# Stack loads of the forgetting stage: alternate partitions and partitions 32 to 95 instead of halves

## Chip, cores and metric

One core of a Trainium2 chip runs a whole decoder layer in float32. The metric is the device time of one execution in microseconds; before the change it is 1514.79 us, the median of three runs (1514.67 to 1516.5).

## What is computed

The layer runs two groups of heads on the same normalised input, an mLSTM (4 heads of 128) and a forgetting attention (8 heads of 64). Their outputs are joined and projected; a cross-attention and an MLP with squared ReLU follow. The change lies in the forgetting attention. For one head, with queries q, keys k, values v, and c the running sum of its log forget gates:

```python
s = jnp.einsum('bqhd,bkhd->bhqk', qi, k) * scale
s = s + (ci[..., :, None] - cT[..., None, :])
s = jnp.where(qpos[:, None] >= kpos[None, :], s, -jnp.inf)
p = jax.nn.softmax(s, axis=-1)
return jnp.einsum('bhqk,bkhd->bqhd', p, v)
```

The sequence has 1024 positions and the model width is 1024.

## The kernel before

Matmuls take float32 operands in two parts, a rounded high part and the remainder, and add three products (`mm3`, lines 186 to 188). `split` (lines 134 and 135, with a scale 137 and 138) makes the two parts: the high one on ScalarE, the low one on VectorE.

Queries and keys of the forgetting heads are projected early (`fx_project`) and stored in HBM as `fqk[which, part, pair, row, position]`. One pair holds two heads, each with 64 rows of 1024 positions, 4 KB a row. The running sums of the gates lie in HBM as `decay`, for each sign and head one row for the high part and one for the low.

For the scores of one head the kernel keeps a stack in SBUF: a tile of 128 partitions and four slots of 1024 columns. There are two stacks, and head `hd` uses `stacks[hd % 2]`.

- Slot 0 (`qs`): the 64 rows of q's high part, and the 64 of its low part.
- Slot 1 (`kh`): k's high part, in both places.
- Slot 2 (`qs2`): the two decay rows of the queries, two rows of ones, q's high part, and zeros elsewhere.
- Slot 3 (`kl`): two rows of ones, the two decay rows of the keys, k's low part, and zeros elsewhere.

A score tile is then two matmuls that contract over all 128 partitions: `qs2` with `kl` (L734) and `qs` with `kh` (L735). The first brings q high times k low and the difference of the running sums, the second the two other products. What stands in which partition does not matter to the sum, as long as both operands agree.

The zeros and ones are written once for each stack, on GpSimd (lines 695 to 697). The rest is loaded for each head: `fx_load` puts eight transfers on the list `coming`, six of 64 rows (256 KB each) from `fqk` and two of 2 rows from `decay`, and `fx_step` issues the next one (line 716). All loads and stores go through SyncE's queue. Completion is counted on eight semaphores in turn, so a transfer is issued only when the one eight places before it has landed.

The first two heads are loaded in one go. From then on work comes in slots (`slot`), one for each tile of values: the transposes of the probabilities (L782), their split (L134, L135), the product with v (L801), the exponentials of earlier scores (L756), one `fx_step`, one `mix_step` (it fetches finished heads from `mix`, L934), the next scores, and then matmuls of other stages that fill PE: keys and values of the cross-attention, and the first part of the output projection (`out_unit`). The weights of the fillers arrive in `wr` (L975) and are cut by `cut_half` (L988, L989). Inside slots, `in_order` fixes the order of instructions on each engine, SyncE included. Outside, in the projection of v (`token_major` with `fv_sink`, which stores to `fvd`, L652) and in the last mLSTM head (causal cut L588, product L541, and the normalised result written through `mix`, L632 and L633), a scheduler orders the work by its own model of times. The buffer `hm`, one load of 2 MB from `hmd` (L1094), is fetched between the projection of v and the slots.

Of the kernel before, what the change touches and what calls it, by code (L numbers as in the profile page):

```python
# [9 lines left out]
F32 = mybir.dt.float32  # L10
# [7 lines left out]
P = 128  # L18
# [7 lines left out]
FXD = 64  # L26
# [18 lines left out]
def hybrid_layer(ctx: ExitStack, tc: tile.TileContext, a: dict, out: bass.AP):  # L45
    nc = tc.nc
    v, s, g = nc.vector, nc.scalar, nc.gpsimd
# [14 lines left out]
    def act(dt=F32R):  # L62
        return sb("act", [P, 8, TH], 7, dt)
# [628 lines left out]
    stacks = []  # L692
    for _ in range(2):
        t = act().rearrange("p a b -> p (a b)").rearrange("p (i c) -> p i c", i=4)
        g.memset(t[0:FXD, 2:4].bitcast(F32), 0.0)
        g.memset(t[32:34, 2].bitcast(F32), 1.0)
        g.memset(t[0:2, 3].bitcast(F32), 1.0)
        stacks.append(t)

    coming = []  # L700
# [1 line left out]
    def fx_load(hd):  # L702

        n, e = divmod(hd, 2)
        hs = stacks[hd % 2]
        rng = slice(e * FXD, e * FXD + FXD)
        lo_, up = slice(0, FXD), slice(FXD, P)
        for rows_, i, which, part in ((lo_, 0, 0, 0), (up, 0, 0, 1), (lo_, 1, 1, 0), (up, 1, 1, 0), (up, 2, 0, 0), (up, 3, 1, 1)):
            coming.append((hs[rows_, i], fqk[which, part, n, rng, :]))
        for at_, i, sign in ((0, 2, 0), (32, 3, 1)):  # L710
            coming.append((hs[at_ : at_ + 2, i], decay[sign, :, MLH + hd, :]))

    def fx_step():
# [116 lines left out]
    def score_parts():  # L830

        for hd in range(FXH):
            for hf in range(2):
                if hf:
                    t = act(F32).rearrange("p a b -> p (a b)").rearrange("p (i c) -> p i c", i=4)
                    rooms[hd, hf] = [t[:, d, : (5 + d) * P] for d in range(4)]
                else:
                    t = [w4((P, 2, TH)) for _ in range(2)]
                    rooms[hd, hf] = [t[d // 2][:, d % 2, : (1 + d) * P] for d in range(4)]
                for d in range(4):  # L840
                    x = Tile(hd, 4 * hf + d, rooms[hd, hf][d])
                    for e in range(len(x.parts)):
                        yield x, e
            if hd + 2 < FXH:
                fx_load(hd + 2)
# [180 lines left out]
    def slot(values, until):  # L1026
# [55 lines left out]
        return x  # L1082

    fx_load(0)
    fx_load(1)
    while coming:
        fx_step()
# [492 lines left out]
    for i in range(2):  # L1580
        t = act()
# [123 lines left out]
```

## Time and profile before

| | |
|---|---|
| median of three runs | 1514.79 us |
| profiled execution | 1516.25 us |
| its span | 1514.5 us |
| granted TensorE clock | 0.997 |
| moved by DMA | 300.91 MB, mean 199 GB/s |
| stacks first filled | 289.9 and 351.5 us |
| forgetting stage | about 370 to 600 us |

An engine's busy time is the union of its instructions' times. "DMA share" is how busy the 16 DMA engines were on average in a window; GB/s is what they moved. In the waits, `A <- B` says that A was idle until B. L12 is line 12 of the kernel.

### The profile page before, as it was taken

Reading aid. Unit: us, or ns where it says so; the run is one execution under the profiler, and the core shown is the slowest. Engines: PE = TensorE matmul, PEld = TensorE weight load, DVE = VectorE, ACT = ScalarE, POOL = GpSimd, SP = SyncE. Lnnn points to the kernel's source line nnn. Section 1 sums busy time; section 2 is a strip of 40 time slices with the busy share of each in tenths; the row PEclk is TensorE's granted clock in tenths of the full one; section 3 lists DMA queues with packets and bytes.
Section 4 is the critical chain, followed back from the end, with each engine's and each line's share of the span. In section 5 each row is a group of like instructions: output and inputs, shape, how many; then the busy total and the mean of one; then the engine's idle time right before and its main releaser. Section 6 shows DMA issues by size and latency. Waiting matters only on the chain.

```text
span 1514.5 us, 21910 instructions
## 1 busy us (share of the span) xinstructions
PE 1496.3 (99%) x7662; PEld 1258.1 (83%) x7662; DVE 1099.9 (73%) x1743; ACT 727.1 (48%) x1360; POOL 511.8 (34%) x543
## 2 busy tenths in 40 slices
PE   9999999999999999999999999999999999999997
PEld 9988888889998888788888878888888888888887
DVE  7766676665788775944457998998996668887665
ACT  7324343334688664634444466666664621122134
POOL 1003030313455441511110044544545366563312
PEclk9999999999999999999999999999999999999998
DMA  6322333435898876843344447776678777776623
GB/s 238 119 78 94 102 105 125 131 129 154 259 249 248 263 261 233 299 145 123 116 149 157 153 141 272 248 264 236 227 260 293 275 278 278 278 271 250 243 90 112
DMA packets 123122, 300.91 MB, mean 199 GB/s; under 512 B 13682, under 2 KB 28332, under 8 KB 116100
## 3 DMA queue, kind: packets, MB, share of 16 engines
q1 hardware_dynamic: 123012, 299.52, 58.3%
q8 instruction: 60, 0.98, 0.3%
q14 instruction: 50, 0.41, 0.1%
HBM read 200.65 MB, written 98.82 MB: 198 GB/s over the span
## 4 chain that ended last, share of the span: by engine, by line
PE 88%; DMA 6%; DVE 3%; issue 1%; ACT 1%; SPq 0%; POOL 0%; DVEq 0%; POOLq 0%; ACTq 0%
PE tp L186 8%; PE tp L187 8%; PE tp L188 8%; PE sc L186 6%; PE sc L188 6%; PE sc L187 6%; PE m L187 5%; PE m L188 5%; PE m L186 5%; PE mm L187 5%; PE mm L186 5%; PE mm L188 5%; PE ov L186 2%; PE ov L187 2%; PE ov L188 2%; PE ov L801 2%
## 5 line engine op out<-in xcount | busy, mean ns | idle before, releaser
L186 PE MATMUL tp<-act,wl 128*128 128x512 f32 (+1 forms) x440 | 172.6, 392 | 0.7 <-ACT row L1398 0.7
L187 PE MATMUL tp<-act,wh 128*128 128x512 f32 (+1 forms) x440 | 172.1, 391 | 0.0
L188 PE MATMUL tp<-act,wh 128*128 128x512 f32 (+1 forms) x440 | 171.7, 391 | 0.0
L135 DVE TENSOR_TENSOR wl<-wr,wh 128x1024 fp32r<-128x1024 f32 (+2 forms) x95 | 125.6, 1322 | 23.4 <-ACT wh L134 23.1
L134 ACT ACTIVATE wh<-wr 128x1024 fp32r<-128x1024 f32 (+2 forms) x95 | 95.6, 1006 | 86.7 <-PE tp L188 36.2
L188 PE MATMUL mm<-act,wh 128*128 128x512 f32 (+1 forms) x332 | 127.4, 384 | 0.0
L186 PE MATMUL mm<-act,wl 128*128 128x512 f32 (+1 forms) x332 | 127.3, 383 | 0.0
L187 PE MATMUL mm<-act,wh 128*128 128x512 f32 (+1 forms) x332 | 127.1, 383 | 0.0
L188 PE MATMUL m<-act,wh 128*128 128x512 f32 (+1 forms) x308 | 117.6, 382 | 0.0
L187 PE MATMUL m<-act,wh 128*128 128x512 f32 (+1 forms) x308 | 117.6, 382 | 0.0
L186 PE MATMUL m<-act,wl 128*128 128x512 f32 (+1 forms) x308 | 117.5, 381 | 0.0
L186 PEld LDWEIGHTS tp<-act,wl 128*128 128x128 f32 x440 | 82.7, 188 | 19.7 <-ACT row L1398 1.2
L188 PEld LDWEIGHTS tp<-act,wh 128*128 128x128 f32 x440 | 82.7, 188 | 19.0
L187 PEld LDWEIGHTS tp<-act,wh 128*128 128x128 f32 x440 | 82.7, 188 | 18.3
L188 PE MATMUL sc<-act,wh 128*128 128x512 f32 (+1 forms) x248 | 96.7, 390 | 0.0
L187 PE MATMUL sc<-act,wh 128*128 128x512 f32 (+1 forms) x248 | 96.7, 390 | 0.0
L186 PE MATMUL sc<-act,wl 128*128 128x512 f32 (+1 forms) x248 | 96.6, 390 | 0.0
L1469 POOL TENSOR_TENSOR z<-wr 128x256 f32<-128x256 f32 x56 | 51.3, 937 | 131.3 <-DMA wr<-w_ff2q 107.9
L134 ACT ACTIVATE wh<-z 128x1024 fp32r<-128x1024 f32 (+1 forms) x54 | 55.5, 1027 | 81.6 <-POOL z L1469 60.5
L135 DVE TENSOR_TENSOR wl<-z,wh 128x1024 fp32r<-128x1024 f32 (+1 forms) x54 | 78.5, 1454 | 10.4 <-ACT wh L134 10.3
L134 ACT ACTIVATE w<-wr 128x768 fp32r<-128x768 f32 (+2 forms) x31 | 25.5, 823 | 106.2 <-PE tp L186 33.4
L188 PEld LDWEIGHTS mm<-act,wh 128*128 128x128 f32 x332 | 62.3, 188 | 12.7
(720 smaller groups left out, 4278.7 us busy)
## 6 DMA issues: line engine op xcount, KB each, us to landing
act<-right SPq DMA_DIRECT2D x49, 1024.0 KB
right<-w SPq DMA_DIRECT2D x56, 256.0 KB
wr<-w_ff2q SPq DMA_DIRECT2D x28, 512.0 KB
right<-r_d SPq DMA_DIRECT2D x49, 256.0 KB
right<-r_e SPq DMA_DIRECT2D x49, 256.0 KB
act<-fqk SPq DMA_DIRECT2D x48, 256.0 KB
wr<-w_in SPq DMA_DIRECT2D x20, 512.0 KB
wr<-w_ff SPq DMA_DIRECT2D x20, 512.0 KB
```

Source lines behind the costliest of these rows:

```text
L134: s.activation(hi, src, AF.Copy)
L135: return v.tensor_tensor(out=lo, in0=src, in1=hi.bitcast(F32), op=ALU.subtract)
L186: nc.tensor.matmul(ps, w[1], x[0], start=first, stop=False, skip_group_check=more)
L187: nc.tensor.matmul(ps, w[0], x[1], start=False, stop=False, skip_group_check=more)
L188: nc.tensor.matmul(ps, w[0], x[0], start=False, stop=last, skip_group_check=more)
L801: nc.tensor.matmul(self.ov[:, c0:], self.fv[:, self.j], t[:, c0:], start=self.j == 0 and t is self.p[1], stop=self.last and t is self.p[0])
L1469: g.tensor_tensor(out=o, in0=x, in1=y, op=op)
```

## The change

The two 64-row parts of slots 0 and 1 go to the even and to the odd partitions instead of to partitions 0 to 63 and 64 to 127. The 64 rows of slots 2 and 3 go to partitions 32 to 95 instead of 64 to 127. The second pair of rows (ones in slot 2, decay in slot 3) moves from partitions 32 and 33 to 96 and 97. The zeros of slots 2 and 3 are written into partitions 0 to 31 and 96 to 127, as two fills of 32 rows, each followed by its two rows of ones; before, they were one fill of 64 rows.

```diff
     for _ in range(2):
         t = act().rearrange("p a b -> p (a b)").rearrange("p (i c) -> p i c", i=4)
-        g.memset(t[0:FXD, 2:4].bitcast(F32), 0.0)
-        g.memset(t[32:34, 2].bitcast(F32), 1.0)
-        g.memset(t[0:2, 3].bitcast(F32), 1.0)
+        for at_, i in ((0, 3), (96, 2)):
+            g.memset(t[at_ : at_ + 32, 2:4].bitcast(F32), 0.0)
+            g.memset(t[at_ : at_ + 2, i].bitcast(F32), 1.0)
         stacks.append(t)
...
-        lo_, up = slice(0, FXD), slice(FXD, P)
-        for rows_, i, which, part in ((lo_, 0, 0, 0), (up, 0, 0, 1), (lo_, 1, 1, 0), (up, 1, 1, 0), (up, 2, 0, 0), (up, 3, 1, 1)):
+        even, odd, mid = slice(0, P, 2), slice(1, P, 2), slice(32, 32 + FXD)
+        for rows_, i, which, part in ((even, 0, 0, 0), (odd, 0, 0, 1), (even, 1, 1, 0), (odd, 1, 1, 0), (mid, 2, 0, 0), (mid, 3, 1, 1)):
             coming.append((hs[rows_, i], fqk[which, part, n, rng, :]))
-        for at_, i, sign in ((0, 2, 0), (32, 3, 1)):
+        for at_, i, sign in ((0, 2, 0), (96, 3, 1)):
             coming.append((hs[at_ : at_ + 2, i], decay[sign, :, MLH + hd, :]))
```

The number, size and order of the loads within a head stay, and no load of `fqk` gains a wait. In the first filling of each stack the second load of decay rows waits for GpSimd too, where only the first did.

The scheduler orders a few instructions anew outside the slots. On GpSimd, at the filling of the second stack (`act` with the number 3180, 3181 in the change; `r_b` and `r_c` belong to the last mLSTM head), before:

```order
L593 TENSOR_TENSOR r_b_2928<-r_c_3115,r_b_2928 128x256
L695 MEMSET act_3180 64x2048
L588 AFFINE_SELECT r_c_3131<-r_c_3131 128x256
L696 MEMSET act_3180 2x1024
L697 MEMSET act_3180 2x1024
L593 TENSOR_TENSOR r_b_2928<-r_c_3131,r_b_2928 128x256
```

and in the change:

```order
L593 TENSOR_TENSOR r_b_2928<-r_c_3115,r_b_2928 128x256
L696 MEMSET act_3181 32x2048 x2
L588 AFFINE_SELECT r_c_3131<-r_c_3131 128x256
L697 MEMSET act_3181 2x1024 x2
L593 TENSOR_TENSOR r_b_2928<-r_c_3131,r_b_2928 128x256
```

One more fill stands ahead of the causal cut (L588), the ones stay behind it. On SyncE, right after the load of `hmd` (about 380 us; numbers of tiles shift by two between the kernels), before:

```order
L632 DMA mix<-r_y_3304 128x512
L633 DMA mix<-r_f_3062 128x512
L652 DMA fvd<-r_c_3699 128x4x128
L652 DMA fvd<-r_b_3728 128x4x128
L716 DMA act_3176<-fqk 64x1024 x3
L975 DMA wr_3890<-w_xv 128x1024
L652 DMA fvd<-r_p_3757 128x4x128
L632 DMA mix<-r_y_3454 128x512
L633 DMA mix<-r_f_2927 128x512
L716 DMA act_3176<-fqk 64x1024
L652 DMA fvd<-r_c_3786 128x4x128
```

and in the change:

```order
L632 DMA mix<-r_y_3306 128x512
L652 DMA fvd<-r_c_3701 128x4x128
L633 DMA mix<-r_f_3062 128x512
L652 DMA fvd<-r_b_3730 128x4x128
L652 DMA fvd<-r_p_3759 128x4x128
L716 DMA act_3176<-fqk 64x1024 x2
L632 DMA mix<-r_y_3456 128x512
L633 DMA mix<-r_f_2927 128x512
L716 DMA act_3176<-fqk 64x1024
L652 DMA fvd<-r_c_3788 128x4x128
L975 DMA wr_3892<-w_xv 128x1024
```

Stores of `fvd` move ahead of the store of `r_f` and of the third stack load, and the load of `w_xv` moves behind three more transfers. On PE some matmuls of the last mLSTM head and the first scores stand later among those of the projection of v. From about 400 us on the queues of both kernels list the same work in the same order.

## The prediction

> **What bounds the kernel now.** I began with the page: the engines' shares, the slices and the chain that ended last.
>
> ```profile
> span 1514.5 us, 21910 instructions
> PE 1496.3 (99%) x7662; PEld 1258.1 (83%) x7662; DVE 1099.9 (73%) x1743; ACT 727.1 (48%) x1360; POOL 511.8 (34%) x543
> DMA  6322333435898876843344447776678777776623
> PE 88%; DMA 6%; DVE 3%; issue 1%; ACT 1%; SPq 0%; POOL 0%; DVEq 0%; POOLq 0%; ACTq 0%
> ```
>
> TensorE (PE) is busy for 99% of the span, so a change that touches no matmul can win only part of 1514.5 - 1496.3 = 18.2 us in which PE does nothing. The DMA slices rise to between 6 and 9 from the eleventh to the seventeenth (one is 37.9 us), which is the forgetting stage with what follows it. The stretches around the change, then (columns: us, busy time of PE, PEld, DVE, ACT, POOL, clock, DMA share, GB/s):
>
> ```profile
> 290.00:310.00 20.00, 20.00 (x103) 16.75 (x102) 12.69 (x29) 6.56 (x11) 6.20 (x6) 1.00 0.63 173
> 350.00:370.00 20.00, 20.00 (x169) 19.88 (x168) 10.08 (x26) 7.59 (x19) 9.61 (x9) 1.00 0.74 182
> 370.00:600.00 230.00, 224.61 (x1456) 200.85 (x1455) 174.48 (x460) 158.69 (x433) 103.84 (x159) 1.00 0.83 253
> ```
>
> From 290 to 310 and from 350 to 370 us, where the stacks are prepared and filled for the first time, PE never stops. In the stage itself (370 to 600) it stops for 230 - 224.61 = 5.4 us, while the DMA engines are busy for 0.83 of the time and yet move only 253 GB/s. The waits of PE name all of these stops:
>
> ```profile
> PE sc L734 <- ACT act L756: 2.1, 1, 2.1
> PE mm L187 <- DMA z<-mix: 2.0, 1, 2.0
> PE tp L782 <- DVE r_b L138: 0.9, 1, 0.9
> PE sc L734 <- ACT w L756: 0.5, 1, 0.5
> ```
>
> The chain in order of time (start, us, what) shows what stands behind the two long ones. The last row of each fence is PE's own from the timeline, with its idle time. The first I call stall A:
>
> ```profile
> 446.39 9.19 DMA wr<-w_xv
> 455.60 0.04 ACT wh L988
> 456.14 0.58 ACT w L134
> 456.72 0.47 ACT act L756 x2
> 457.23 0.50 PE sc L734
> ...
> 457.23 0.50 PE L734 MATMUL sc<-act 128*128 128x512 f32 x1 [2.06 <-ACT act L756]
> ```
>
> A weight load issued at 446.39 needs 9.19 us. ScalarE works in a fixed order, its cut of these weights (L988) stands ahead of the exponentials (L756), and so the scores (L734) find no free bank. The second, stall B:
>
> ```profile
> 491.15 7.64 DMA act<-mix
> 498.81 8.47 DMA z<-mix
> 507.32 0.51 PE mm L187
> ...
> 507.32 0.51 PE L187 MATMUL mm<-z,wh 128*128 128x512 f32 x1 [1.95 <-DMA z<-mix]
> ```
>
> PE itself waits for the last piece of the mixed heads, 8.47 us under way. Both stalls are DMA latency, and both in stretches where the DMA engines have no free time.
>
> **The change, part by part.** *The loads.* Each head brings six loads of 64 rows from `fqk`, 256 KB each; 36 of the 48 fall into the stage, as its row for 370 to 600 us says first below. What one costs where little else runs, against whole-tile traffic, stands in two windows, with what was issued in the first and in the second:
>
> ```profile
> L716 SPq DMA_DIRECT2D act<-fqk x36: 444/550/1882, 387.0 to 524.8; - x36
> 354.00:360.00 6.00, 6.00 (x53) 6.00 (x53) 2.55 (x6) 2.29 (x6) 1.93 (x3) 1.00 1.04 221
> 533.00:540.00 7.00, 7.00 (x37) 5.79 (x36) 5.65 (x15) 4.00 (x13) 4.02 (x7) 1.00 1.02 346
> act<-fqk SPq DMA_DIRECT2D x6, 256.0 KB
> act<-mix SPq DMA_DIRECT2D x4, 256.0 KB
> ```
>
> Both windows have DMA engines that never rest (1.04 and 1.02), but the one made of loads into half the partitions moves 221 GB/s, the one made of loads and stores over all 128 partitions 346. So 262,144 bytes take 1.19 us in the first way and 0.76 in the second, 0.43 us less. The middle loads (partitions 32 to 95) and the alternate ones (every second partition) occur nowhere in this trace. Their price is bounded by 0.76 if the whole spread of the tile is what counts, 1.19 if only the number of rows counts, and above that only if a stride itself costs something, which no row suggests. I take 0.76 for both kinds, since what sets the two windows apart is how far the rows spread over the tile: 36 x 0.43 = 15.4 us of queue time less, out of 0.83 x 230 = 191 us.
>
> [...]
>
> *Stall A.* The queue around it (SyncE's issues; then the window in which the load is served):
>
> ```profile
> 438.29 1.89 SPq L716 DMA_DIRECT2D act<-fqk  x3
> ...
> 445.29 0.41 SPq L849 DMA_DIRECT2D w<-fvd  x1
> 445.74 0.54 SPq L716 DMA_DIRECT2D act<-fqk  x1
> 446.39 1.42 SPq L975 DMA_DIRECT2D wr<-w_xv  x1
> 447.86 0.45 SPq L716 DMA_DIRECT2D act<-fqk  x1
> 449.00:456.00 7.00, 6.17 (x43) 5.34 (x41) 5.03 (x12) 3.77 (x11) 1.77 (x3) 1.00 1.00 226
> ```
>
> One stack load is just ahead of the weights and one behind (three more were issued from 438.29 on), yet the whole window, with its 128-partition loads, crawls at 226 GB/s. I read this as loads on half the tile holding up the writing of the others. By count, A shortens by one load, 0.43 us. By rate, 7 us x 226 GB/s = 1.58 MB would take 4.6 us at 346 GB/s, 2.4 us earlier, more than the 2.06 us that PE is idle. I take the rate, because a window at 226 is nearest to the stack loads' own 221: A goes, -2.1 us (bounds -0.4 and -2.1).
>
> *Stall B.* Between 484 and 498.8 us five stack loads are issued ahead of the piece that PE waits for:
>
> ```profile
> L716 SPq DMA_DIRECT2D act<-fqk x5: 450/558/617, 486.7 to 497.5; - x5
> 484.00:508.00 24.00, 22.05 (x155) 20.20 (x154) 19.12 (x53) 16.89 (x48) 11.65 (x19) 1.00 1.00 281
> ```
>
> By count 5 x 0.43 = 2.15 us earlier; by rate 24 x (1 - 281/346) = 4.5 us. Both exceed the 1.95 us of idle: B goes, -1.95 us. What is late next after both: nothing that a row shows. DVE is busy for 174.5 of 230 us and ACT for 158.7, and in both stalls they wait behind the same load.
>
> *The zeros and ones.* On GpSimd (columns: busy us, mean ns):
>
> ```profile
> L695 POOL MEMSET act<- 64x2048 f32 x2 | 3.6, 1808 | 0.0
> L696 POOL MEMSET act<- 2x1024 f32 x2 | 1.9, 952 | 0.1
> ```
>
> Half the columns take half the time although 2 rows stand against 64, so the time goes by columns, and two fills of 32 rows cost 2 x 1.81 instead of 1.81 us: 1.8 us more for each stack. Behind the second stack's fill, GpSimd has the causal cut (L588) of the last mLSTM tile, and DVE, ACT and PE (L541) wait for that in turn. The fill sits in the window from 350 to 370, where PE is never idle, and the scheduler has put those matmuls later on PE, so other projection matmuls cover it: 0. If that cover were gone, it would cost at most 1.8 us, once.
>
> *The waits.* Now the second load of the decay rows also waits for GpSimd, as the first does today. Behind it on SyncE stand a store of `fqk` and the load of `w_fv` for the first stack, and a store of `fvd` for the second, each up to 1.8 us later. PE is idle for 0 us from 290 to 310 and from 350 to 370, and those queues empty sooner by 6 x 0.43 = 2.6 us: 0.
>
> *The matmuls* have the same count and shapes, and both operands permute alike: 0. *The order* near 380 us: stores of `fvd` go ahead of the last store of `mix` and of stack loads, a weight load falls behind. The store that leads to the third stall (0.9 us) keeps its place right behind the big load of `hmd`: 0, bounds -0.9 and +0.9.
>
> *Sum.* -2.06 - 1.95 = -4.0 us. The profiled execution took 1516.25 us (span 1514.5 and 1.75 around it), and would take 1512.2; it lies 1.5 above the median of the runs, 1514.79, from which I forecast 1510.8. The three runs lie within 1.8 us, about 0.12%, so 0.2% (3.0 us) is about what a measurement can tell from no change.
>
> **The rivals.** *Only the middle loads get faster (17%).* [...]
>
> *The waits come back (13%).* PE gains and then waits for DVE or ACT, which are busy for 0.76 and 0.69 of the stage. Half of A and B and the 0.9 us at most would return, -1.0: 1513.8. Against: PE has no other stop over 0.5 us in 230.
>
> *Strided rows are slow (15%), the other side.* If a load of alternate partitions took twice today's price, 2.37 us, A's weights would be held by the three such loads issued from 438 us on and B's piece by four: 3 x 1.19 - 0.43 = +3.1 and 4 x 1.19 - 0.43 = +4.3, and PE waits longer by both: +7.4, 1522.2. With 7 loads in these two queues it costs 3 us from 0.55 us more a load, a price of 1.74. For it: the kind of load is new. Against: every row stays one piece of 4 KB, and their number is the same.
>
> **How the numbers follow.** The forecast has 55%, the rivals 17, 13 and 15. Within the forecast the lower end is all four stops gone, 1514.8 - 5.4 = 1509.4, and 0.6 for the scatter of runs; the middle-only and returning cases reach 1513.8 and the scatter of 1.8 above it about 1516. The range 1508.8 to 1516.0 leaves out the slow case. Faster by over 0.2% needs 3.0 of the 4.0 us: most of the forecast's share and a little of the first rival's, 0.52. Slower takes the third, 0.15. Within 0.2% is the rest, 0.33.
>
> **What would show it.** In the changed kernel's windows the first fills of the second stack should run near 346 GB/s, the load of `wr<-w_xv` before L988 should take under 7 us, PE's waits should lack both 2 us entries, and the stage should lose about 4 us. An unchanged 221 GB/s with one wait left would speak for the first rival, new waits on DVE or ACT for the second, longer latencies of `z<-mix` for the third. The forecast is wrong if the loads are faster and PE still stops for as long.

## The result, and the profile after

The changed kernel takes 1511.86 us (median of 14 runs, 1510.88 to 1513.41) against 1514.73 us before on the same chip (14 runs, 1512.43 to 1518.28). The ratio is 0.9979, with a 95% interval from 0.9971 to 0.9987: 2.9 us less, between 2.0 and 4.4. The forecast of 1510.8 lies 1.1 us under the median. The profiled execution took 1512.88 us (before 1516.25), 3.4 us less; it lies 1.0 us above its median, the one before 1.5 above, which is the difference between 3.4 and 2.9.

The page of the changed kernel: the span, TensorE's busy time, the DMA slices, and the shares of the chain that ended last.

```profile
span 1511.1 us, 21913 instructions
PE 1496.5 (99%) x7662; PEld 1258.6 (83%) x7662; DVE 1100.0 (73%) x1743; ACT 727.0 (48%) x1360; POOL 514.6 (34%) x545
DMA  6322333435777877934344447777678777776623
PE 95%; DMA 2%; DVE 1%; ACT 1%; issue 1%; SPq 0%; POOLq 0%; POOL 0%; DVEq 0%; ACTq 0%
```

PE does the same 1496 us of work, and does nothing for 14.6 us of the span instead of 18.2. The first four DMA slices of the stage (the eleventh to the fourteenth) fall from 8, 9, 8, 8 to 7, 7, 7, 8, and the share of DMA in the chain from 6% to 2%. The windows that the prediction read, in the changed kernel (columns: us, busy time of PE, PEld, DVE, ACT, POOL, clock, DMA share, GB/s):

```profile
354.00:360.00 6.00, 6.00 (x53) 6.00 (x52) 1.64 (x6) 1.46 (x4) 4.03 (x5) 1.00 0.85 272
370.00:400.00 30.00, 27.99 (x210) 25.90 (x210) 19.30 (x61) 15.67 (x47) 8.32 (x16) 1.00 0.82 268
400.00:600.00 200.00, 200.00 (x1264) 177.98 (x1263) 158.08 (x404) 143.90 (x388) 94.51 (x143) 1.00 0.76 255
370.00:600.00 230.00, 227.99 (x1471) 203.87 (x1471) 177.38 (x464) 159.57 (x434) 102.83 (x159) 1.00 0.76 257
449.00:456.00 7.00, 7.00 (x54) 6.58 (x52) 5.96 (x15) 6.14 (x16) 2.83 (x4) 1.00 0.93 315
484.00:508.00 24.00, 24.00 (x164) 21.95 (x164) 20.39 (x57) 18.07 (x51) 12.78 (x21) 1.00 0.87 310
```

From 400 to 600 us PE no longer stops at all. In the whole stage it stops for 2.0 us instead of 5.4, and the DMA share falls from 0.83 to 0.76. The window of stall A moves 315 GB/s instead of 226, that of stall B 310 instead of 281 with idle time to spare (share 0.87 instead of 1.00). The queue's own row from 370 to 600 us (packets, MB, share of the 16 engines' time), before:

```profile
q1 hardware_dynamic: 29868, 57.91, 82.7%
```

and in the changed kernel:

```profile
q1 hardware_dynamic: 30301, 58.69, 75.9%
```

Of 230 us, 82.7 - 75.9 = 6.8 points are 15.6 us. What is left of PE's waits in the stage (us in total, times, longest):

```profile
PE tp L782 <- DVE r_b L138: 1.1, 1, 1.1
PE sc L734 <- ACT w L756: 0.5, 1, 0.5
PE sc L734 <- ACT act L756: 0.4, 1, 0.4
```

Both 2 us entries are gone. At stall A's place, the timeline of SyncE shows the issue of the weights,

```profile
449.29 0.52 SPq L975 DMA_DIRECT2D wr<-w_xv  x1
```

and that of ScalarE the cut which waits for them:

```profile
454.68 0.63 ACT L988 ACTIVATE wh<-wr 128x512 fp32r<-128x512 f32 x1 [0.42 <-DMA wr<-w_xv]
```

The weights are there 5.4 us after their issue instead of 9.19. ScalarE still waits for them, but for 0.42 us, and PE has work meanwhile. At stall B's place, the instructions on the tile `z` (durations min/median/max in ns, first and last start in us):

```profile
L934 SPq DMA_DIRECT2D z<-mix x1: 577/577/577, 495.8 to 495.8; - x1
L186 PE MATMUL mm<-z,wl x1: 394/394/394, 504.1 to 504.1; 128*128 128x512 f32 x1
```

The last piece of the mixed heads is issued at 495.8 instead of 498.81 us, and PE goes through the matmuls on `z` from 504.1 on without a wait. The fills on GpSimd cost what was worked out (busy us, mean ns):

```profile
L696 POOL MEMSET act<- 32x2048 f32 x4 | 7.2, 1802 | 0.1
L697 POOL MEMSET act<- 2x1024 f32 x4 | 3.8, 947 | 0.2
```

### The profile page after: what moved, and what is told of

Its sections match the earlier page's. It is cut to its first block, busy times and chain, and to the rows that moved or that the text cites. A ratio compares the mean times of both kernels' runs of the same rounds, so it can differ in the third digit from the quotient of the medians.

```text
span 1511.1 us, 21913 instructions
## 1 busy us (share of the span) xinstructions
PE 1496.5 (99%) x7662; PEld 1258.6 (83%) x7662; DVE 1100.0 (73%) x1743; ACT 727.0 (48%) x1360; POOL 514.6 (34%) x545
## 4 chain that ended last, share of the span: by engine, by line
PE 95%; DMA 2%; DVE 1%; ACT 1%; issue 1%; SPq 0%; POOLq 0%; POOL 0%; DVEq 0%; ACTq 0%
PE tp L186 8%; PE tp L187 8%; PE tp L188 8%; PE sc L186 6%; PE sc L188 6%; PE sc L187 6%; PE m L188 6%; PE m L187 6%; PE m L186 6%; PE mm L186 6%; PE mm L187 6%; PE mm L188 6%; PE ov L801 2%; PE ov L186 2%; PE ov L187 2%; PE ov L188 2%
## 5 line engine op out<-in xcount | busy, mean ns | idle before, releaser
L186 PEld LDWEIGHTS tp<-act,wl 128*128 128x128 f32 x440 | 82.7, 188 | 19.7 <-ACT row L1398 1.2
L188 PEld LDWEIGHTS tp<-act,wh 128*128 128x128 f32 x440 | 82.7, 188 | 19.0
L187 PEld LDWEIGHTS tp<-act,wh 128*128 128x128 f32 x440 | 82.7, 188 | 18.3
```

Source lines behind the costliest of these rows:

```text
L186: nc.tensor.matmul(ps, w[1], x[0], start=first, stop=False, skip_group_check=more)
L187: nc.tensor.matmul(ps, w[0], x[1], start=False, stop=False, skip_group_check=more)
L188: nc.tensor.matmul(ps, w[0], x[0], start=False, stop=last, skip_group_check=more)
```

## The experiments

Each kernel ran in five rounds beside the kernel before. The first four shared one chip, where before took 1515.38 us (35 runs); the last two shared another, where it took 1515.26 (19 runs).

**Fills only.** The four small fills and their order are kept, the loads stay halves. By their order on every engine, this kernel and the changed one are the same.

```diff
-        g.memset(t[0:FXD, 2:4].bitcast(F32), 0.0)
-        g.memset(t[32:34, 2].bitcast(F32), 1.0)
-        g.memset(t[0:2, 3].bitcast(F32), 1.0)
+        for at_, i in ((0, 3), (32, 2)):
+            g.memset(t[at_ : at_ + 32, 2:4].bitcast(F32), 0.0)
+            g.memset(t[at_ : at_ + 2, i].bitcast(F32), 1.0)
```

> All loads as before the change; only the zeros are written in two fills of 32 rows (partitions 0 to 31 and 32 to 63), each with its ones. Every engine then issues in the order of the changed kernel. Theory (the gain comes from the spread of the loads; the extra fill and the new order around it only cost): stalls A and B stay at about 2 us each, and the kernel is slower than before by 0.5 to 1.5 us, what the changed kernel gave back before 400 us. Rival (the new order moves the transfers clear of each other, and that is the gain): A and B are gone or shorter, 2 to 3 us faster than before.

Measured: 1515.97 us (12 runs), ratio 1.0004 [0.9994, 1.0014]; the profiled execution 1516.39. Its waits of PE:

```profile
PE sc L734 <- ACT act L756: 3.4, 5, 1.2
PE mm L187 <- DMA z<-mix: 1.2, 1, 1.2
```

Its windows before and after 400 us:

```profile
370.00:400.00 30.00, 26.59 (x198) 24.60 (x196) 18.95 (x57) 15.16 (x46) 8.34 (x16) 1.00 0.81 255
400.00:600.00 200.00, 197.93 (x1251) 175.51 (x1252) 155.28 (x402) 142.91 (x388) 94.46 (x144) 1.00 0.83 253
```

Two pieces of its chain (start, us, what):

```profile
373.96 6.04 DMA r_a<-facd
380.80 4.22 DMA r_a<-facd
```

The new order alone wins nothing that can be measured. It does not leave the stops where they were, though, which I had not expected: 3.4 us of PE's idle time now lie before 400 us, where loads of the last mLSTM head take 6.04 and 4.22 us, and 2.1 us after it. The total is 230 - 224.51 = 5.5 us, as before (5.4). What is left at the places of A and B:

```profile
457.99 0.51 PE L734 MATMUL sc<-act 128*128 128x512 f32 x1 [0.58 <-ACT act L756]
507.32 0.50 PE L187 MATMUL mm<-z,wh 128*128 128x512 f32 x1 [1.24 <-DMA z<-mix]
```

The same two pieces of the chain in the changed kernel, with the same order:

```profile
374.89 4.80 DMA r_a<-facd
380.49 3.35 DMA r_a<-facd
```

They are shorter by 2.1 us, and the stop behind them (L734) is the 0.4 us in its waits above. So in these two profiles with half loads the order decides where PE waits for the queue, and hardly how long in all.

**One fill.** The changed loads, with a single fill of slots 2 and 3 over all 128 partitions. On every engine this has the order of before, apart from the fills themselves. The diff is against the changed kernel.

```diff
+        g.memset(t[:, 2:4].bitcast(F32), 0.0)
         for at_, i in ((0, 3), (96, 2)):
-            g.memset(t[at_ : at_ + 32, 2:4].bitcast(F32), 0.0)
             g.memset(t[at_ : at_ + 2, i].bitcast(F32), 1.0)
```

> All loads as in the change; the zeros are one fill of all 128 partitions, so that PE, DVE, ACT and SyncE issue in the order of the kernel before. Theory (spread): A and B gone, and without the give-back before 400 us: 3.5 to 4.2 us faster than before, 0.5 to 1.3 faster than the change. Rival (order): within 1 us of before, A and B both there.

Measured: 1511.54 us (11 runs, 1510.28 to 1512.71), ratio 0.9974 [0.9966, 0.9983]; profiled 1511.63. Its waits of PE in the stage:

```profile
PE tp L782 <- DVE r_b L138: 1.3, 1, 1.3
PE sc L734 <- ACT w L756: 0.5, 1, 0.5
```

Its window after 400 us:

```profile
400.00:600.00 200.00, 200.00 (x1257) 177.77 (x1256) 157.09 (x400) 142.89 (x385) 93.93 (x143) 1.00 0.75 251
```

The spread of the loads alone, in the old order, brings the gain: 3.8 us by the medians. The two shapes of the fill are not told apart, since the intervals overlap. The weights of stall A, their issue on SyncE and their cut on ScalarE:

```profile
446.37 0.54 SPq L975 DMA_DIRECT2D wr<-w_xv  x1
452.87 0.63 ACT L988 ACTIVATE wh<-wr 128x512 fp32r<-128x512 f32 x1
```

The cut does not wait, so the weights were there within 6.5 us of an issue at the same time as before, when they took 9.19: at least 2.7 us sooner. The prediction had 0.43 by count and 2.4 by rate. The window from 449 to 456 us moves only 253 GB/s here, at a share of 0.70: once the queue is no longer full, its rate is not the 346 of the estimate.

**Only the middle loads.** Slots 0 and 1 in halves as before, slots 2 and 3 at partitions 32 to 95 (12 of the stage's 36 loads). The fills, the decay rows and the order are the changed kernel's, and the diff is against it.

```diff
-        even, odd, mid = slice(0, P, 2), slice(1, P, 2), slice(32, 32 + FXD)
+        even, odd, mid = slice(0, FXD), slice(FXD, P), slice(32, 32 + FXD)
```

> Slots 2 and 3 as in the change (partitions 32 to 95, two fills), slots 0 and 1 in halves as before; order of the changed kernel. One third of the loads is spread. Theory by rate (the mixed queue runs at the pace of its slowest loads): A mostly gone, since the fifth and sixth load are the ones beside it, B still 1.5 us, so 1 to 2 us faster than before after the give-back. Theory by count: A 1.6 us, B 1.5, within 0.5 us of before. Rival (order): as fast as the change.

Measured: 1512.51 us (11 runs), ratio 0.9981 [0.9971, 0.9991]; profiled 1512.34. Its waits of PE in the stage:

```profile
PE tp L782 <- DVE r_b L138: 1.1, 1, 1.1
PE sc L734 <- ACT act L756: 0.5, 1, 0.5
PE sc L734 <- ACT w L756: 0.5, 1, 0.5
```

Its windows of A and B:

```profile
449.00:456.00 7.00, 7.00 (x53) 6.57 (x53) 6.14 (x15) 6.28 (x18) 2.83 (x5) 1.00 0.90 310
484.00:508.00 24.00, 24.00 (x164) 21.86 (x163) 18.96 (x54) 17.63 (x50) 11.57 (x19) 1.00 0.99 309
```

The queue's row from 370 to 600 us:

```profile
q1 hardware_dynamic: 30287, 58.63, 78.8%
```

With a third of the loads spread, PE stops at neither place. The order of the changed kernel already shortens both, so the kernel to compare with is the one with fills only, where A was 0.58 and B 1.24 us. The matmul that waited for the last piece there is this one here:

```profile
504.31 0.40 PE L187 MATMUL mm<-z,wh 128*128 128x512 f32 x1
```

It starts 3.0 us earlier, where counting the one middle load ahead of it gives 0.43. At A the 0.58 us are too little to tell count from rate. The time, 2.9 us less than before, is beyond both expectations (within 0.5 us by count, 1 to 2 us by rate).

**Only the alternate loads.** Slots 0 and 1 in even and odd partitions, slots 2 and 3 at partitions 64 to 127 as before, with the fills and the order of before, against which the diff stands.

```diff
-        lo_, up = slice(0, FXD), slice(FXD, P)
-        for rows_, i, which, part in ((lo_, 0, 0, 0), (up, 0, 0, 1), (lo_, 1, 1, 0), (up, 1, 1, 0), (up, 2, 0, 0), (up, 3, 1, 1)):
+        even, odd, up = slice(0, P, 2), slice(1, P, 2), slice(FXD, P)
+        for rows_, i, which, part in ((even, 0, 0, 0), (odd, 0, 0, 1), (even, 1, 1, 0), (odd, 1, 1, 0), (up, 2, 0, 0), (up, 3, 1, 1)):
```

> Slots 0 and 1 in alternate partitions, slots 2 and 3 in 64 to 127 as before, zeros as before; order of the kernel before. Two thirds of the loads are spread. Theory: B gone or below 0.3 us (four of the five loads ahead of it are 0.43 us shorter, 1.7 us), A between 0.8 and 2.06 us, as the loads beside it are the slow kind; 2 to 3 us faster than before. If a stride cost as much as a half (the rival of the prediction), B stays and the kernel is within 0.5 us of before. In the first filling of the second stack four loads should run near 0.7 us and two near 1.2.

Measured: 1512.81 us (11 runs), ratio 0.9987 [0.9977, 0.9997]; profiled 1512.06. Its waits of PE (the two longest):

```profile
PE tp L782 <- DVE r_b L138: 1.1, 1, 1.1
PE sc L734 <- ACT act L756: 0.6, 1, 0.6
```

The same two windows:

```profile
449.00:456.00 7.00, 6.41 (x43) 5.55 (x42) 5.93 (x14) 5.24 (x15) 2.77 (x4) 1.00 0.81 237
484.00:508.00 24.00, 24.00 (x160) 21.81 (x159) 18.96 (x54) 18.21 (x51) 11.46 (x19) 1.00 0.97 305
```

The queue's row:

```profile
q1 hardware_dynamic: 29916, 58.20, 79.0%
```

A stride of two costs nothing that shows: B's window, where four of the five stack loads are alternate ones, moves 305 GB/s and has no stop. Beside A the loads are middle ones, which are halves here; A shrinks from 2.06 to 0.6 us all the same, but does not go. A count of the three alternate loads issued from 438 us on (3 x 0.43 = 1.3 us) would fit these 1.5 us; what fails is counting only the load just ahead. What a single load costs in the first filling can't be read off: the window from 354 to 360 us moves 225 GB/s at a share of 0.82.

The queue's rows put a price on each kind. Per megabyte, the queue was busy for 0.827 x 230 / 57.91 = 3.28 us before, 2.97 in the changed kernel, 3.09 with the middle loads and 3.12 with the alternate ones. With fills only it is 3.28 again (82.6% for 57.91 MB), so the order is not what lowers it. Over 58 MB that is 18 us less, and 11 and 9 us for the parts, 20 together. So both placements relieve the queue, and the 12 middle loads brought at least as much as the 24 alternate ones. How much of it falls to the stack loads and how much to the transfers beside them, no row splits. In the kernel before, the first four loads of a head go to the lower and the upper half in turn, and the last two both to the upper; that two neighbours on one half cost more would fit, but no run separates it.

**The third stop.** What is left in the stage is one stop of 1.1 to 1.3 us at L782. ScalarE stands before it, waiting for the store of `r_y` to `mix`, which is queued behind the 2 MB load of `hmd`. One kernel takes the version with one fill and issues that load after the store, another does the same to the kernel before.

```diff
-    facd = dram.tile([MLH, T], F32, name="facd")
+    facd = dram.tile([MLH, T], F32, name="facd"); stored = []
...
-            load(mix[hf, 1, :, hd], yl.bitcast(F32))
+            stored.append(load(mix[hf, 1, :, hd], yl.bitcast(F32)))
...
-    load(hm.bitcast(F32), hmd)
+    with tc.issue_after(stored[-2].ins): load(hm.bitcast(F32), hmd)
```

> All loads as in the change, one fill of 128 partitions, and the 2 MB load of hmd issued behind the first stores of the last mLSTM head instead of ahead of them; PE's order is that of the kernel before. Theory: the stop of about 1.1 to 1.3 us left at 392 us is ScalarE waiting for the buffer of the store of r_y, which stands behind the 2 MB load; it goes or falls below 0.4 us, and the kernel is 4.5 to 5.3 us faster than before, about 1 us faster than with one fill alone. Rival (the store of fvd that now stands behind the load takes its place, since its buffer is needed next): a stop of about 1 us stays, and the time is within 0.4 us of the kernel with one fill.

Measured: 1511.44 us (9 runs, 1510.13 to 1511.58), ratio 0.9973 [0.9963, 0.9984]; profiled 1510.63. ScalarE's longest wait from 384 to 400 us with one fill alone:

```profile
ACT r_y L137 <- DMA mix<-r_y: 4.4, 1, 4.4
```

The longest in this kernel:

```profile
ACT r_b L137 <- PE tp L188: 2.4, 1, 2.4
```

PE's waits in this kernel's stage:

```profile
PE sc L734 <- ACT w L756: 0.4, 1, 0.4
PE tp L782 <- DVE r_b L138: 0.4, 1, 0.4
PE sc L734 <- ACT act L756: 0.2, 1, 0.2
```

The wait for the store is gone and the stop shrinks from 1.3 to 0.4 us. More than the load moved: on ScalarE, VectorE and SyncE the scheduler also put the split of `r_y` (L137, L138) and its two stores ahead of work that they followed before, and the split starts at 383.5 us instead of 391.5. So the wait for that store made most of the stop; whether the place of the load alone would remove it is not shown. With fills only, where ScalarE waited just 0.96 us for the store, the stop was 0.4 us too, with the load in its old place. The profiled execution is 1.0 us shorter than with one fill alone, but the medians differ by 0.1 us, and the gain is not shown. This is the fastest kernel measured; it beats the kernel before clearly and the changed kernel only by the point estimate.

> The kernel before with its loads and fills, and only the load of hmd issued behind those stores. Theory (the stops are independent): A and B stay, the stop of 0.9 us at 392 us goes, 0.5 to 1 us faster than before. Rival (the stops feed one another: the tail of the 2 MB load is what keeps the queue full up to A): A shortens too, 2 us or more faster than before.

Measured: 1515.08 us (11 runs), ratio 0.9998 [0.9987, 1.0009]; profiled 1515.08. Its long wait of PE in the stage and that of the third stop:

```profile
PE sc L734 <- ACT act L756: 3.2, 3, 2.4
PE tp L782 <- DVE r_b L138: 0.4, 1, 0.4
```

Its window after 400 us:

```profile
400.00:600.00 200.00, 196.82 (x1238) 173.99 (x1237) 154.52 (x398) 142.27 (x385) 93.47 (x142) 1.00 0.85 254
```

Here, too, the third stop falls, from 0.9 to 0.4 us, and the medians show nothing. Stall A became longer (2.4 instead of 2.06), while B is nearly gone in this profile: neither expectation was quite met. That would fit A being set by when the queue delivers (PE arrives sooner and waits longer), but one profile does not show it. With an interval of some 1.6 us either way, a gain of half a microsecond can't be excluded.

## Why the prediction came out right, step by step

- **Both stalls are DMA latency, and the half loads make it:** shown. With the order of before and the loads spread, both go and PE never stops between 400 and 600 us (busy for 200.00 of 200 us with one fill); with the changed order and half loads nothing is gained (1515.97 us, a ratio of 1.0004). The term of -4.0 us for both is what the profiles of before and of one fill show at these two places. That the two places stood for the kernel's usual loss was in part luck: with fills only they held 0.58 and 1.24 us, while the total of the stage was the same.
- **By rate, not by count:** counting the load just ahead is refuted. A's weights come at least 2.7 us sooner with one fill, and B's matmul 3.0 us sooner with the middle loads alone, where the count gives 0.43 each. The lower bound for A (-0.4) was far too careful. The rate came near at A (2.4), but that the window's rate is the right price is not shown in general.
- **0.43 us a load, 15.4 us of queue time:** the queue's row gives 15.6 us, or 18 at equal bytes. The share by kind was wrong: I had priced both the same, and each middle load relieved the queue by more (11 us for 12 against 9 us for 24).
- **First fills at 346 GB/s:** missed. The window moves 272 GB/s, but at a share of 0.85, where before it was full at 1.04. The DMA engines have idle time in it now; per busy time it is 272 / 0.85 = 320.
- **Fills on GpSimd +1.8 us a stack, at no cost:** the time by columns is right (1802 ns for 32 rows, 1808 for 64 before), and the kernel with fills alone has no measurable loss, though its interval allows up to 2 us. A single fill would have avoided them (from 290 to 370 us GpSimd is busy for 22.78 us with one fill, for 22.98 before and 25.03 in the changed kernel).
- **Order, third stop and waits around the stage, each 0 in the sum:** this is the term that was mis-sized. In the profiled executions the third stop grew from 0.9 to 1.1 us and a stop of 0.4 came at L734. So the stage won 3.4 instead of 4.0 us. PE is also idle for 0.8 us between 290 and 370, against 0.1 us before (busy for 79.88 of 80). The window:

```profile
290.00:370.00 80.00, 79.21 (x503) 71.02 (x502) 46.85 (x88) 30.57 (x58) 25.03 (x28) 1.00 0.47 148
```

The two waits in it:

```profile
PE sc L186 <- DVE r_b L589: 0.4, 1, 0.4
PE mm L186 <- DVE r_p L641: 0.3, 1, 0.3
```

These 0.7 us are made up elsewhere in the span, where nothing was changed, so that the profiles differ by 3.4 in all. The two waits stand at 332 and 335 us, between the two fillings, and fills alone, with the same order, lacks them; whether they belong to the change stays open. The rest of the distance, from 3.4 to the 2.9 us of the medians, lies in the profiled executions: the forecast took its 4.0 us of stops from one that was 1.5 us above the median, and subtracted them in full from the median. How many of these stops an execution at the median has, no run shows. Against the medians the forecast is not refuted: its ratio of 0.9974 lies inside the interval.

- **The rivals.** Only the middle loads faster: refuted by the alternate loads alone (B gone, the queue's price down to 3.12 us per MB). The queue's price falls with either placement (3.09 and 3.12 us per MB against 3.28). Waits come back: only in the small way just told, since PE has 200.00 of 200 us after 400. Strided rows slow: refuted by the same run.

## What to carry to other kernels

Where a transfer fills half of the partitions, choose the half so that it spreads over the tile, when the computation lets rows be permuted: here the queue's price fell from 3.28 to 2.97 us per MB with both placements, it costs no instruction (21910 before and with one fill), and the transfers queued beside it gain too (stall A's weights were there within 6.5 us with one fill, instead of 9.19). Counting only the loads just ahead of a late transfer priced this far too low (0.43 us against 2.7 or more); the rate of the window in which it is under way came nearer. And judge a change of order by the idle time of a whole stage: with half loads, stops that left one place turned up at others (fills only: 5.5 us in all, 5.4 before).

## What the runs showed that I had not expected

The scatter from run to run goes with the half loads. The kernel before ran from 1511.7 to 1519.9 us in 35 runs and from 1512.67 to 1520.23 in 19, fills only from 1512.84 to 1519.36 (12 runs), and before with `hmd` later from 1512.56 to 1517.54 (11 runs). All kernels with some or all loads spread stay within 3.2 us (9 to 14 runs each): the changed kernel 1510.88 to 1513.41, one fill 1510.28 to 1512.71, and with `hmd` later 1510.13 to 1511.58. The stops that the queue sets vary with the execution, so the two stalls of before, 2.06 and 1.95 us in its one profile, are a sample: fills only had five stops of up to 1.2 us at L734, and the kernel before with `hmd` later one of 2.4. The total of PE's stops in the stage moves less: 5.4, 5.5 and 4.2 us in the three profiles with half loads, 1.0 to 2.2 in those with spread ones.
